# Twelve places in SBUF for the weights' two parts: each ring buffer starts at its own byte within 128

## The chip, the cores and the metric

One core of one Trainium2 chip. The metric is the device time of one execution in microseconds; runs of the same kernel are compared by their medians.

## The reference

Two layers on one sequence of 256 positions and a width of 1024, all in float32. Each layer adds a mixer, an MLP and a gated embedding to the running sum `x`:

```python
for i in range(DEPTH):                      # DEPTH = 2
    if i % 2 == 0:                          # layer 0: dilated attention, 16 heads, 3 groups
        x = x + dilated_attention(rms_norm(x, a_norm), a_w_qkv, a_q_gain, a_k_gain, a_w_o)
    else:                                   # layer 1: mLSTM with up and down projection
        x = x + mlstm_mixer(rms_norm(x, b_norm), b_w_up, ..., b_w_down)
    x = x + jnp.square(jax.nn.relu(rms_norm(x, mlp_norm[i]) @ mlp_w1[i])) @ mlp_w2[i]
    gate = jax.nn.sigmoid(rms_norm(x, ple_norm[i]) @ ple_w_gate[i])
    x = x + gate * (p[i] @ ple_w_proj[i])
```

The weights are 138 pieces of 128 x 2048 float32 (1 MB each), read once.

## The kernel before

**Three products for one.** Weights and activations are each split into two float32r parts, h (rounded) and l (the rest), and each 128 x 128 tile of weights is multiplied three times: h by h, h by l, l by h. In the streams of the MLPs, gates and projections (`stream`) the weights are the stationary operand, loaded anew before every matmul, and 256 columns of activations move (lines 335, 336 and 337, in this order). In `qkv_block` it is the other way about: 128 columns of the activations are stationary and 512 columns of weights move (lines 503 to 505).

**The weights' way.** A unit of 1 MB is loaded by one DMA (`raw`, three buffers) four units ahead. `split` cuts it into four slots of 512 columns: ScalarE copies a slot to the high part `hi` (line 180), VectorE subtracts to get `lo` (line 181). Both go to rings of twelve buffers of 2048 bytes a partition, some eleven slots ahead of use. A slot is 12 matmuls of 256 columns, or 6 of 512. Slot number `4*u + c` runs on over all units, so it returns to the same buffer every twelve slots.

**The order of the streams.** 36 units of `qkv` with the attention between them, then by units: proj0 1, woA and woB 4, w1_0 16, w2_0 16, gate0 4, xm 8, z0 to z3 8, wd0 4, proj1 1, wd1 4, w1_1 16, w2_1 16, gate1 4; 102 units of 48 matmuls of 256 columns. Small matmuls of attention and mLSTM (`fill`) stand between slots.

**Where the operands lie.** A pool's tiles stand one after another, each rounded up to 32 bytes (the 16-byte tile `rx` takes 32), and pools stand one after another; SBUF is full to its last hundred bytes in the mLSTM. The layout of the program before, as the byte of a partition's address within 128 at which a tile starts:

| tile | byte | it is read in |
|---|---|---|
| all twelve `hi`, all twelve `lo` | 64 | all streams |
| `raw` | 0 | splitting |
| `hA` (`hh`, `hl`), `hW` | 0 | qkv, w1_0, xm, z, wd1, gate1 |
| `hid` (`hidh`, `hidl`) of both MLPs, `hB` | 0 | w2_0, w2_1, w1_1, wd0 |
| `oT` (`oTh`, `oTl`) | 64 | woA, woB |
| `hG` (`hGh`, `hGl`), `pT` of layer 0, `x` | 96 | gate0, proj0 |
| `pT` of layer 1 | 32 | proj1 |

Weights and moving operand are thus 64 bytes apart in most streams, 0 in woA and woB, 96 (or -32) in gate0 and proj0, and 32 in proj1. The two lines `gap0` and `gap1` of 64 bytes make the weights' 64.

Of the kernel before, what the change touches and what calls it, by code (L numbers as in the profile page):

```python
# [10 lines left out]
F32 = mybir.dt.float32  # L11
F32R = mybir.dt.float32r
I32 = mybir.dt.int32
AF = mybir.ActivationFunctionType
# [4 lines left out]
D, S, P = 1024, 256, 128  # L19
# [9 lines left out]
UC = 2048  # L29
HU = 512  # L30
# [102 lines left out]
def build(tc, a):  # L133
    nc = tc.nc
    ctx = ExitStack()
    with ctx:
        _build(ctx, tc, nc, a)


def _build(ctx, tc, nc, a):  # L140
    def pool(n, b=1, c=ctx, **k):
        if "space" not in k:
            k["reuse_waits"] = "tile"
        return c.enter_context(tc.tile_pool(name=n, bufs=b, **k))

    base = pool("base")
    rawp = pool("raw", 3)

    pool("gap0").tile([P, 16], F32, name="gap0")
    hip, lop = pool("hi", 3 * UC // HU), pool("lo", 3 * UC // HU)  # L150
    pool("gap1").tile([P, 16], F32, name="gap1")
    psa = pool("psa", 3, space=PSUM)
    pst = pool("pst", 2, space=PSUM)
    pss = pool("pss", 2, space=PSUM)
# [3 lines left out]
    act = nc.scalar.activation  # L158
# [4 lines left out]
    raw, hi, lo = {}, {}, {}  # L163
# [6 lines left out]
    def split(u, c, back=None):  # L170
        if u >= NU:
            return
        n = u, c * 512 // HU
        if c * 512 % HU == 0:
            hi[n] = hip.tile([P, HU], F32R, name="hi")
            lo[n] = lop.tile([P, HU], F32R, name="lo")
        s = slice(c * 512, c * 512 + 512)
        d = slice(c * 512 % HU, c * 512 % HU + 512)
        with tc.high_priority(offset=-(BACK if back is None else back)):
            act(hi[n][:, d], raw[u][:, s], AF.Copy)  # L180
            dve.tensor_tensor(lo[n][:, d], raw[u][:, s], hi[n][:, d], op=ALU.subtract)  # L181
# [31 lines left out]
    def open_slot():  # L213
        u, c = divmod(clock[0], 4)
        while ahead[0] < clock[0] + lead[0]:
            ahead[0] += 1
            split(*divmod(ahead[0], 4))
        if c == 0:
            dma(u + LD)
        return u, c  # L220
# [11 lines left out]
    ones = base.tile([P, P], F32, name="ones")  # L232
# [6 lines left out]
                nc.sync.dma_start(x[:, 2 * j:2 * j + 2], a["x"][:, 2 * j:2 * j + 2])  # L239
            nc.sync.dma_start(raw[u][:, j * 512:(j + 1) * 512], a["w"][u, :, j * 512:(j + 1) * 512])  # L240
    nc.sync.dma_start(ident, a["eye"])
    first = base.tile([P, 1], F32, name="first")
    act(first, ones[:, 0:1], AF.Exp)

    warm = psm.tile([P, 512], F32, name="sm")
    for _ in range(WARM):
# [5 lines left out]

    hA = [base.tile([P, KT, S], F32R, name=f"h{n}") for n in "hl"]
    sqp = pool("sq", 2)

    class Stats:

# [25 lines left out]
    def rsqrt(y, v, shape):  # L283
        t = sqp.tile(shape, F32, name="rt")
        dve.tensor_scalar(y.bitcast(I32), v.bitcast(I32), -0.5, RSQRT_MAGIC, op0=ALU.mult, op1=ALU.add)
        for _ in range(3):
            dve.tensor_tensor(t, y, y, op=ALU.mult)
            dve.scalar_tensor_tensor(t, t, -0.5, v, op0=ALU.mult, op1=ALU.mult)
            dve.scalar_tensor_tensor(y, t, 1.5, y, op0=ALU.add, op1=ALU.mult)
# [62 lines left out]
    atp = pool("attn", c=actx)  # L352
# [5 lines left out]
    for j in range(4):  # L358
        for k in (2 * j, 2 * j + 1):
            scaled(hA, k, x[:, k], pr("gA"))  # L360
        split(0, j, 0)
    for j in range(4):
        split(1, j, 0)
# [13 lines left out]

    def first_stats():
        st.total()
        sw = atp.tile([P, P], F32, name="sw")  # L380
        dve.tensor_copy(sw[:, 0:64], st.s[:, 192:256])
        dve.tensor_copy(sw[:, 64:128], st.s[:, 0:64])
        for n, t in ((2, st.s[:, 64:192]), (3, sw)):
            mm(st.ps[:, 256 + n:257 + n], t, ones[:, 0:1], start=True, stop=True)
        v = atp.tile([P, 4], F32, name="v4")
        dve.tensor_scalar(v, st.ps[:, 256:260], 1.0 / D, EPS, op0=ALU.mult, op1=ALU.add)
        dve.tensor_scalar(epsx, v[:, 0:2], EPS, None, op0=ALU.mult)
        rsqrt(rx, v, [P, 4])

    def wrap():  # L390
        for n in range(2):
            act(hW[n][:, :, 0:64], hA[n][:, :, 192:256], AF.Copy)
            act(hW[n][:, :, 64:128], hA[n][:, :, 0:64], AF.Copy)

    at(0, first_stats)
    at(8, wrap)

# [283 lines left out]
    mp = pool("mlp0", c=mctx)  # L681
    hid = [mp.tile([P, 32, S], F32R, name=f"hid{n}") for n in "hl"]
# [11 lines left out]
    mp = pool("gate0", c=mctx)  # L694
# [279 lines left out]

    mctx = ExitStack()
    mp = pool("mlp1", c=mctx)
    hid = [mp.tile([P, 32, S], F32R, name=f"hid{n}") for n in "hl"]
    gst = Stats()
    mlp(1, x, hB, mst, hid, mp, hA, "gP1", gst)

# [98 lines left out]
```

## Time and profile before

| | |
|---|---|
| median of three runs | 910.12 us (909.98 to 912.25) |
| the profiled execution's own time | 912.26 us |
| its span, first to last instruction | 910.5 us |
| mean granted clock of TensorE | 0.997 of 2.4 GHz |
| TensorE busy, weight loads busy | 894.8 us (98%), 833.9 us (92%) |
| VectorE busy, ScalarE busy | 659.2 us (72%), 568.5 us (62%) |
| HBM read | 148 MB, 164 GB/s over the span |

Matmuls are pipelined, so the time of one (280 ns for 256 columns) is not what it adds to the span. What it adds is the distance between its start and the next one's, called its spacing below: in the timeline, where every matmul has a row, it is the last start less the first, divided by the rows between.

### The profile page before, as it was taken

The numbers are of one execution on the slowest core, as the hardware profiler recorded it, in microseconds if no ns is written. First come the engines' busy times: TensorE is split into PE (matmuls) and PEld (weight loads), VectorE is DVE, ScalarE is ACT, GpSimd is POOL, SyncE is SP. The second block draws the span as 40 slices with busy tenths as digits, with TensorE's granted clock in tenths as the row PEclk, the third lists the DMA queues.
The fourth block names the chain that finished last, engine by engine and source line by source line (L and its number), as shares of the span: only waits on it lengthen the run. The fifth ranks groups of instructions, "written<-read, shape, count | busy, mean of one in ns | idle before, by whom it ended". The sixth has DMA issues, their size and how long they took to land.

```text
span 910.5 us, 17609 instructions
## 1 busy us (share of the span) xinstructions
PE 894.8 (98%) x6924; PEld 833.9 (92%) x6924; DVE 659.2 (72%) x1409; ACT 568.5 (62%) x1055; POOL 39.4 (4%) x77
## 2 busy tenths in 40 slices
PE   8799999999999999999999999999999999999997
PEld 7687787777889999999999989999999999999997
DVE  6966877857876977765666987668898766656664
ACT  7567576676675766655555777678766666655552
POOL 0410000000000000000000343000000000000000
PEclk9999999999999999999999999999999999999999
DMA  8744434445343455555555433442256555555521
GB/s 305 282 140 147 178 130 150 143 141 180 132 148 137 149 188 185 190 183 188 187 191 175 154 130 134 140 140 93 94 197 223 175 187 188 188 183 188 190 102 47
DMA packets 23122, 150.23 MB, mean 165 GB/s; under 512 B 2560, under 2 KB 3200, under 8 KB 5632
## 3 DMA queue, kind: packets, MB, share of 16 engines
q1 hardware_dynamic: 23040, 149.12, 47.4%
q8 instruction: 54, 0.88, 0.4%
q14 instruction: 28, 0.23, 0.1%
HBM read 148.06 MB, written 1.05 MB: 164 GB/s over the span
## 4 chain that ended last, share of the span: by engine, by line
PE 92%; DVE 6%; issue 1%; ACT 1%; DMA 0%; SPq 0%; ACTq 0%
PE acc L335 21%; PE acc L336 21%; PE acc L337 20%; PE acc L503 6%; PE acc L505 6%; PE acc L504 6%; DVE lo L181 2%; PE tp L455 1%; PE tp L556 1%; PE sm L574 1%; PE sc L531 1%; PE tp L745 1%; PE tp L755 1%; PE sc L886 1%; PE sc L763 1%
## 5 line engine op out<-in xcount | busy, mean ns | idle before, releaser
L181 DVE TENSOR_TENSOR lo<-raw,hi 128x512 fp32r<-128x512 f32 x552 | 375.3, 690 | 169.2 <-ACT hi L180 163.8
L180 ACT ACTIVATE hi<-raw 128x512 fp32r<-128x512 f32 x552 | 338.7, 628 | 216.8 <-PE acc L336 194.1
L335 PE MATMUL acc<-hh,hi 128*128 128x256 f32 x640 | 182.5, 285 | 0.2 <-ACT hh L302 0.2
L336 PE MATMUL acc<-hl,hi 128*128 128x256 f32 x640 | 179.8, 281 | 0.4 <-DVE hl L303 0.3
L337 PE MATMUL acc<-hh,lo 128*128 128x256 f32 x640 | 179.7, 281 | 0.0
L337 PE MATMUL acc<-hidh,lo 128*128 128x256 f32 x512 | 143.3, 280 | 0.0
L336 PE MATMUL acc<-hidl,hi 128*128 128x256 f32 x512 | 143.3, 280 | 0.0
L335 PE MATMUL acc<-hidh,hi 128*128 128x256 f32 x512 | 143.1, 279 | 0.0
L336 PEld LDWEIGHTS acc<-hl,hi 128*128 128x128 f32 x640 | 121.7, 190 | 1.0 <-DVE hl L303 0.8
L335 PEld LDWEIGHTS acc<-hh,hi 128*128 128x128 f32 x640 | 120.7, 189 | 1.5 <-issue 0.7
L337 PEld LDWEIGHTS acc<-hh,lo 128*128 128x128 f32 x640 | 120.3, 188 | 0.0
L503 PE MATMUL acc<-hi,hh 128*128 128x512 f32 x264 | 109.9, 417 | 0.0
L504 PE MATMUL acc<-lo,hh 128*128 128x512 f32 x264 | 104.4, 396 | 0.8 <-DVE lo L181 0.8
L505 PE MATMUL acc<-hi,hl 128*128 128x512 f32 x264 | 104.8, 397 | 0.0
L336 PEld LDWEIGHTS acc<-hidl,hi 128*128 128x128 f32 x512 | 96.3, 188 | 0.0
L335 PEld LDWEIGHTS acc<-hidh,hi 128*128 128x128 f32 x512 | 96.2, 188 | 0.0
L337 PEld LDWEIGHTS acc<-hidh,lo 128*128 128x128 f32 x512 | 96.0, 188 | 0.0
L336 PE MATMUL acc<-hBl,hi 128*128 128x256 f32 x320 | 89.9, 281 | 0.0
L335 PE MATMUL acc<-hBh,hi 128*128 128x256 f32 x320 | 89.8, 281 | 0.0
L337 PE MATMUL acc<-hBh,lo 128*128 128x256 f32 x320 | 89.5, 280 | 0.0
L335 PEld LDWEIGHTS acc<-hBh,hi 128*128 128x128 f32 x320 | 60.3, 188 | 0.3 <-issue 0.3
L336 PEld LDWEIGHTS acc<-hBl,hi 128*128 128x128 f32 x320 | 60.1, 188 | 0.0
(258 smaller groups left out, 1382.7 us busy)
## 6 DMA issues: line engine op xcount, KB each, us to landing
raw<-w SPq DMA_DIRECT2D x136, 1024.0 KB, 4.9
raw<-w SPq DMA_DIRECT2D x8, 256.0 KB, 5.9
x<-x SPq DMA_DIRECT2D x4, 256.0 KB, 5.6
pj<-rep SPq DMA_DIRECT2D x1, 896.0 KB, 6.7
out<-u SPq DMA_DIRECT2D x3, 256.0 KB, 2.4
pT<-p SPq DMA_DIRECT2D x2, 256.0 KB, 3.9
nd<-nd SPq DMA_DIRECT2D x1, 384.0 KB, 5.6
out<-u SPq DMA_DIRECT2D x2, 128.0 KB, 1.9
```

The costliest lines, as they stand in the source:

```text
L180: act(hi[n][:, d], raw[u][:, s], AF.Copy)
L181: dve.tensor_tensor(lo[n][:, d], raw[u][:, s], hi[n][:, d], op=ALU.subtract)
L335: mm(acc[:, q], wh, h, start=first, stop=False, skip_group_check=n > 1)
L336: mm(acc[:, q], wh, l, start=False, stop=False, skip_group_check=n > 1)
L337: mm(acc[:, q], wl, h, start=False, stop=last, skip_group_check=n > 1)
L455: nc.tensor.transpose(ps[:, pair, b * P:(b + 1) * P], n[:, b, ty * 256 + pair * P:ty * 256 + (pair + 1) * P], ident)
L503: mm(accs[b], hh, wh, start=(k == 0), stop=False)
L504: mm(accs[b], hh, wl, start=False, stop=False)
L505: mm(accs[b], hl, wh, start=False, stop=(k == 7))
L531: mm(ps[:, 0:256], q[r, pair, tb], k[r, pair], start=first, stop=last)
L556: nc.tensor.transpose(psf[:, k * P:(k + 1) * P], pe[:, k * P:(k + 1) * P], ident)
L574: mm(out, VT[qt, 0][:, n, cols], pt[:, n * P:(n + 1) * P], start=(n == 0), stop=False, skip_group_check=True)
```

## The change

The two pools of twelve buffers become 24 pools of one buffer, with gap tiles between them, so that the buffers of a ring no longer start at one byte within 128. `RING` lists the intended pairs (byte of `hi`, byte of `lo`), counted from the end of `raw`; slot n uses pair n modulo 12. In the second MLP a gap of 32 bytes is put between `hidh` and `hidl`. To make room, the tile `first` (4 bytes, a slot of 32) goes: the early `Exp`, which has ScalarE load its table, now writes a tile `v` of the pool `sq` and stands after the warm-up matmuls in the program; and `sw` (512 bytes) takes the place of `t2` by a common tag.

```diff
-    pool("gap0").tile([P, 16], F32, name="gap0")
-    hip, lop = pool("hi", 3 * UC // HU), pool("lo", 3 * UC // HU)
-    pool("gap1").tile([P, 16], F32, name="gap1")
+    RING = ((64, 64), (64, 0), (64, 32), (64, 96), (0, 64), (32, 32), (96, 96), (32, 96), (96, 32), (48, 48), (80, 80), (0, 0))
+    ring = {}
+    at_ = 0
+    for part in range(2):
+        for n in sorted(range(len(RING)), key=lambda n: RING[n][part]):
+            gap = (RING[n][part] - at_) % 128
+            if gap:
+                pool(f"gap{part}{n}").tile([P, gap // 4], F32, name="gap")
+            at_ += gap
+            ring[part, n] = pool(("hi", "lo")[part] + str(n))
+    pool("gap").tile([P, (-at_) % 128 // 4], F32, name="gap")
...
-            hi[n] = hip.tile([P, HU], F32R, name="hi")
-            lo[n] = lop.tile([P, HU], F32R, name="lo")
+            hi[n], lo[n] = (ring[part, (4 * u + c) % len(RING)].tile([P, HU], F32R, name=nm) for part, nm in enumerate(("hi", "lo")))
...
-    first = base.tile([P, 1], F32, name="first")
-    act(first, ones[:, 0:1], AF.Exp)
...
     sqp = pool("sq", 2)
+    act(sqp.tile([P, 2], F32, name="v"), ones[:, 0:2], AF.Exp)
...
-        sw = atp.tile([P, P], F32, name="sw")
+        sw = atp.tile([P, P], F32, name="sw", tag="t2")
...
-    hid = [mp.tile([P, 32, S], F32R, name=f"hid{n}") for n in "hl"]
+    hid = []
+    for n in "hl":
+        if n == "l":
+            mp.tile([P, 8], F32, name="gap")
+        hid.append(mp.tile([P, 32, S], F32R, name=f"hid{n}"))
```

## Rows read from the trace of the kernel before

**Rows 1.** The page: busy time by engine, and the chain that ended last.

```profile
PE 894.8 (98%) x6924; PEld 833.9 (92%) x6924; DVE 659.2 (72%) x1409; ACT 568.5 (62%) x1055; POOL 39.4 (4%) x77
...
PE 92%; DVE 6%; issue 1%; ACT 1%; DMA 0%; SPq 0%; ACTq 0%
```

**Rows 2.** Busy time by stretch: us, then each engine's busy us and instructions.

```profile
100.00:200.00 100.00, 100.00 (x662) 79.85 (x659) 73.02 (x190) 65.06 (x134) 0.00 (x0) 1.00 0.43 148
...
400.00:450.00 50.00, 50.00 (x427) 50.00 (x426) 29.98 (x49) 24.97 (x42) 0.00 (x0) 1.00 0.54 182
```

**Rows 3.** TensorE's waits: who waited for whom, total us, times, longest.

```profile
PE tp L455 <- DVE nqk L447: 4.9, 1, 4.9
...
PE acc L504 <- DVE lo L181: 0.8, 1, 0.8
```

**Rows 4.** TensorE's timeline in w2_0, first and last of 147 matmuls.

```profile
409.76 0.28 PE L335 MATMUL acc<-hidh,hi 128*128 128x256 f32 x1
...
426.96 0.28 PE L337 MATMUL acc<-hidh,lo 128*128 128x256 f32 x1
```

**Rows 5.** The same in z1 (27 matmuls) and in z3 (26 matmuls).

```profile
594.00 0.28 PE L335 MATMUL acc<-hh,hi 128*128 128x256 f32 x1
...
597.07 0.28 PE L337 MATMUL acc<-hh,lo 128*128 128x256 f32 x1
...
627.11 0.28 PE L336 MATMUL acc<-hl,hi 128*128 128x256 f32 x1
...
629.95 0.28 PE L337 MATMUL acc<-hh,lo 128*128 128x256 f32 x1
```

**Rows 6.** The same in woB, 26 matmuls.

```profile
299.83 0.28 PE L336 MATMUL acc<-oTl,hi 128*128 128x256 f32 x1
...
302.83 0.28 PE L337 MATMUL acc<-oTh,lo 128*128 128x256 f32 x1
```

**Rows 7.** The same in gate0, two stretches: 26 and 97 matmuls.

```profile
486.22 0.28 PE L336 MATMUL acc<-hGl,hi 128*128 128x256 f32 x1
...
489.22 0.28 PE L337 MATMUL acc<-hGh,lo 128*128 128x256 f32 x1
...
497.17 0.28 PE L337 MATMUL acc<-hGh,lo 128*128 128x256 f32 x1
...
508.37 0.28 PE L337 MATMUL acc<-hGh,lo 128*128 128x256 f32 x1
```

**Rows 8.** The same in proj1, 37 matmuls.

```profile
673.47 0.29 PE L337 MATMUL acc<-pT,lo 128*128 128x256 f32 x1
...
677.73 0.28 PE L337 MATMUL acc<-pT,lo 128*128 128x256 f32 x1
```

**Rows 9.** The same in qkv, 512 columns: 25 matmuls, and 8 with hW.

```profile
191.43 0.40 PE L505 MATMUL acc<-hi,hl 128*128 128x512 f32 x1
...
196.92 0.39 PE L505 MATMUL acc<-hi,hl 128*128 128x512 f32 x1
...
73.59 0.40 PE L505 MATMUL acc<-hi,hWl 128*128 128x512 f32 x1
...
75.23 0.39 PE L503 MATMUL acc<-hi,hWh 128*128 128x512 f32 x1
```

**Rows 10.** Groups by line: busy us, mean ns; idle before, releaser.

```profile
L181 DVE TENSOR_TENSOR lo<-raw,hi 128x512 fp32r<-128x512 f32 x552 | 375.3, 690 | 169.2 <-ACT hi L180 163.8
...
L654 DVE TENSOR_TENSOR hidl<-s,hidh 128x512 fp32r<-128x512 f32 x32 | 22.2, 693 | 3.2
```

**Rows 11.** DMA issues: times, KB each, median us to landing.

```profile
raw<-w SPq DMA_DIRECT2D x8, 256.0 KB, 5.9
x<-x SPq DMA_DIRECT2D x4, 256.0 KB, 5.6
```

**Rows 12.** ScalarE's first instructions.

```profile
0.73 1.28 ACT L243 ACT_TABLE_LOAD   x1 [0.73 <-PEq L1071]
...
5.05 0.91 ACT L302 ACTIVATE hh<-x,prm 128x256 fp32r<-128x256 f32 x2 [2.83 <-DMA x<-x]
```

## The prediction

> **What bounds the kernel now.** I read the page first. TensorE's matmuls cover 98% of the span and the chain that ended last is 92% PE [rows 1]; the longest wait of TensorE for another engine is 4.9 us, the one for a weight part 0.8 us [rows 3]. So the end is set by how fast matmuls follow each other, and VectorE, ScalarE and the DMA queue matter only where they would make TensorE wait. A busy share of 98% hides the quantity that counts here, so I went to the timeline and took spacings: last start less first start, by the rows between. In w2_0 it is (426.96 - 409.76) / 146 = 117.8 ns [rows 4]; the window 400 to 450 us holds 427 matmuls, 50 us / 427 = 117.1 ns [rows 2], less by the matmuls in flight at its ends.
>
> The reader is to compare spacings of one and the same instruction, 128 x 128 weights and 256 moving columns, in different streams:
>
> - weights and moving operand 64 bytes apart: 117.8 ns [rows 4], but also 3.07 / 26 = 118.1 ns in z1 and 2.84 / 25 = 113.6 ns in z3, with the same tiles [rows 5];
> - 0 apart (`oT`): 3.00 / 25 = 120.0 ns [rows 6];
> - 96 apart (`hG`): first 3.00 / 25 = 120.0 ns, after a break in the stream 11.20 / 96 = 116.7 ns [rows 7];
> - 32 apart (`pT` of proj1): 4.26 / 36 = 118.3 ns [rows 8].
>
> At 2.4 GHz, the clock granted nearly everywhere, 256 columns are 106.7 ns; every stream pays 7 to 13 ns on top. In qkv, 512 columns (213.3 ns) take 5.49 / 24 = 228.8 ns, and 1.64 / 7 = 234.3 ns with `hW` [rows 9]. What goes with the differences is the place of the operands; and since one place gives two values (z1, z3), also a state into which a stream falls and in which it stays until something breaks it: w2_0 holds its 117.8 ns through 147 rows.
>
> The Trainium skill speaks against any such effect: "TensorE: Matmul & The Clock Gate", in "Step-by-step: what each phase is for", says that matmul and weight load read SBUF through two independent ports and that loading the next weights takes no read bandwidth from the running matmul; "SBUF — State Buffer", under "Who interferes with whom", that PE waits for nobody there. By that rule the change is worth 0. The trace does not agree, by 113.6 against 120.0 ns for one shape at one clock [rows 5, 6].
>
> **Which places the change really gives.** A slot of a pool is rounded up to 32 bytes, so the gaps of 16 bytes before the entries 48, 64, 80 and 96 take 32 each. I count the layout through. `first` gives back 32 bytes, so `hh`, `raw` and the start of the ring move to 96 within 128, and the activations with them; only distances can matter if anything does. By slot the pairs (`hi`, `lo`) become, from that start: (96,32), (96,64), (96,96) twice, (0,32), (32,96) four times, (64,0), (0,64) twice. So `hi` lies at 0 three times, at 32 four, at 64 once, at 96 four times; `lo` at 0 once, 32 twice, 64 three times, 96 six times. The pair (64,64) of before is gone. If the 16-byte gaps are taken as written instead, the twelve pairs of the list hold; the mean below moves by some 0.2 ns, within the bounds.
>
> **The streams of 256 columns.** A price for each distance, from the rows: 120.0 at 0; 118.3 at 32; at 96 the mean over its two stretches, (25 x 120.0 + 96 x 116.7) / 121 = 117.4; at 64 the middle of 117.8 and 113.6, 115.7, since a slot of twelve matmuls between two others may land in either state. Of three matmuls two run beside the loading of a `hi` tile and one beside a `lo` tile. Mean for `hi`: (3 x 120.0 + 4 x 118.3 + 115.7 + 4 x 117.4) / 12 = 118.2. For `lo`: (120.0 + 2 x 118.3 + 3 x 115.7 + 6 x 117.4) / 12 = 117.3. A triple: (2 x 118.2 + 117.3) / 3 = 117.9 ns. That prices add in this way when the distance changes inside a triple is not shown by any row; it is my choice between the ends below.
>
> - 76 units (w1, w2, wd, gate1; 3648 matmuls) are at 117.8 now: +0.1 ns, +0.4 us.
> - 16 units (xm, z; 768) are some at 113.6, some at 118.1 now [rows 5], middle 115.9: +2.0 ns, +1.5 us.
> - woA and woB (192) are at 120.0; `oT` lies 64 from the others, so each price moves on by 64: (2 x 117.5 + 118.4) / 3 = 117.8: -0.4 us.
> - gate0, proj0, proj1 (288), at 117.4 to 118.3 now: +0.1 us.
> - The second MLP's gap shifts the distance of `lo` to `hidl` by 32 in a third of w2_1, 256 matmuls: `lo` would stand at 117.2 for 117.3: nothing.
>
> Sum +1.6 us. Ends: all 4896 matmuls at 113.6 would be -15.3 - 1.8 - 1.2 - 1.1 = -19 us; all at 120.0 would be 8.0 + 3.1 + 0.7 = +12 us.
>
> **The qkv streams.** 864 matmuls, 48 of them with `hW`. The same distance of 64 bytes shows 228.8 and 234.3 ns [rows 9], so here distance within 128 alone does not tell the price. Ends: 0, and 816 x 5.5 ns = +4.5 us. I take a fifth of that, +0.9 us, since nearly all of qkv runs at the lower value now.
>
> **The other edits.** VectorE's subtraction is 690 ns with `raw` at 0 and `hi` at 64 and 693 ns for the same operation with both inputs at 0 [rows 10]: its place costs nothing, and both splitting engines idle behind TensorE anyway (busy 72% and 62%). `raw` moves to an address of 32 within 64; `x` lies so already, and its DMA of 256 KB lands in 5.6 us against 5.9 for `raw`'s [rows 11]: nothing, with a 1 MB load issued four units (over 20 us) ahead as cover; were it gone, each unit would wait for its load. The early `Exp` keeps its place as ScalarE's first instruction: the table load ends at 2.0 us, and the next instruction waits for `x` until 5.05 us [rows 12]; without that cover it would cost 1.3 us. `sw` is last read long before `t2` is written by slot 52: nothing. Buffers are handed back one by one as before, twelve slots apart: no new wait.
>
> **Sum.** +1.6 + 0.9 = +2.5 us. On the profiled execution's own 912.26 us that is 914.8; on the median of the runs, 910.12, which lies 2.1 us below it, 912.6 us. A measurement of this kernel can tell some 0.3%, 2.7 us, from no change, so the forecast stands at the edge between the same and slower.
>
> **Rivals.**
>
> - *The held state breaks (the other side).* Place: the 3648 matmuls that stand at 117.8 in undisturbed streams. Now nothing disturbs them; after, the distance jumps every twelve matmuls and inside each triple. In xm and z, where small matmuls break the stream, z3 sits at 113.6 [rows 5], and gate0 fell from 120.0 to 116.7 after breaks [rows 7]. Against it: z1 stayed at 118.1 between breaks, and 113.6 is seen only at a distance of 64, which few buffers keep. Price: at 115.7 everywhere -2.1 x 3648 = -7.7 us, 902.5; in full -15 us, 895. It decides once the mean of the ring is below 117.1 ns (-0.7 x 3648 = -2.7 us).
> - *Jumps cost more than any one place.* Then most slots go to 120 ns: +12 us, 922; with qkv at its upper end 926. At half of it 917. For it: 120.0 stands wherever distance is 0, and the ring holds three such `hi`. Against: no stream shows more than 120.0 for long.
> - *The places do not matter in sum, or the change does not do what it says:* within 1 us, 910 to 911. For it: distances 32, 64 and 96 all average 116 to 118 ns.
>
> **How the numbers follow.** My forecast's case, a mean of 117.4 to 118.6 ns and so -1 to +6 us, gets 0.5; its own range is 909 to 916. The held state breaking gets 0.25, dearer jumps 0.15, no effect 0.1. Slower by over 0.3%: half of the first case and the third, 0.41; faster: 0.25; the rest, 0.34, within. The range leaves out the far half of the second case and the far end of the third: 903 to 919.
>
> **What would show it.** Take the spacing by slot in w1 and w2: right is a pattern that returns every twelve slots, between some 114 and 120 ns, slots with `hi` and the moving tile 0 apart the slowest; a window of 50 us in w2 holds 426 to 428 matmuls again. Wrong would be one flat value in all slots, or slots under 113 or over 121. The xm and z streams should lose their runs at 113.6 ns. DMA, the subtraction's 690 ns and the start should stay. The prediction fails if the prices do not add across a triple: then the mean can lie anywhere between 113.6 and 120.

## The result, and the profile after

The changed kernel takes 917.17 us (916.25 to 917.49, three runs) against 910.12 for the one before: 1.0074 times as long [1.0056, 1.0091], slower by 7.05 us. Its profiled execution took 916.25 us with a span of 914.4 us against before's 910.5; unrounded it is 914.45 against 910.45, 4.0 us more. So of the 7 us between the medians a little over half stands in the two traces; the rest lies between the runs of either kernel and is taken up below. Two executions of the kernel before in later sessions, of 1093 and 4981 us, are slow ones and are left out everywhere.

The page of the changed kernel, busy time and the chain that ended last:

```profile
PE 899.2 (98%) x6924; PEld 836.8 (92%) x6924; DVE 659.9 (72%) x1409; ACT 569.5 (62%) x1055; POOL 41.5 (5%) x77
...
PE 95%; DVE 4%; ACT 1%; DMA 1%; issue 0%; SPq 0%; ACTq 0%
```

TensorE has 4.4 us more of busy time for the same 6924 matmuls [rows 1]. Its waits did not grow; the two that answer to [rows 3]:

```profile
PE tp L461 <- DVE nqk L453: 4.8, 1, 4.8
...
PE acc L510 <- DVE lo L188: 0.7, 1, 0.7
```

The subtraction did not grow either (690 ns before [rows 10]), and the 136 loads of 1 MB land in 4.9 us both times. Only the loads of 256 KB at the start land a little later than in [rows 11], 6.2 for 5.9 us (6.8 in a second trace of before):

```profile
L188 DVE TENSOR_TENSOR lo<-raw,hi 128x512 fp32r<-128x512 f32 x552 | 375.9, 691 | 171.6 <-ACT hi L187 166.8
...
raw<-w SPq DMA_DIRECT2D x136, 1024.0 KB, 4.9
raw<-w SPq DMA_DIRECT2D x8, 256.0 KB, 6.2
x<-x SPq DMA_DIRECT2D x4, 256.0 KB, 5.7
```

What is left is the spacing of the matmuls. Busy time by stretch, in qkv and in w2_0: 10 matmuls fewer in 100 us and 2 fewer in 50 us than in [rows 2], at a granted clock of 1.00 both times (the prediction had 426 to 428 in w2; it is 425).

```profile
100.00:200.00 100.00, 100.00 (x652) 79.25 (x653) 73.14 (x189) 64.57 (x133) 0.00 (x0) 1.00 0.43 148
400.00:450.00 50.00, 50.00 (x425) 50.00 (x424) 29.73 (x48) 25.04 (x42) 0.00 (x0) 1.00 0.53 182
```

TensorE's timeline of the changed kernel, first and last row of four stretches that answer to [rows 4, 5, 6, 9]: qkv (25 matmuls), woB (32), w2_0 (146), z3 (17).

```profile
192.04 0.39 PE L511 MATMUL acc<-hi,hl 128*128 128x512 f32 x1
...
197.61 0.39 PE L511 MATMUL acc<-hi,hl 128*128 128x512 f32 x1
...
298.73 0.28 PE L343 MATMUL acc<-oTh,lo 128*128 128x256 f32 x1
...
302.35 0.28 PE L341 MATMUL acc<-oTh,hi 128*128 128x256 f32 x1
...
409.73 0.27 PE L343 MATMUL acc<-hidh,lo 128*128 128x256 f32 x1
...
426.89 0.28 PE L341 MATMUL acc<-hidh,hi 128*128 128x256 f32 x1
...
630.78 0.28 PE L342 MATMUL acc<-hl,hi 128*128 128x256 f32 x1
...
632.68 0.28 PE L343 MATMUL acc<-hh,lo 128*128 128x256 f32 x1
```

Read as spacings: qkv 5.57 / 24 = 232.1 ns (228.8 before), woB 3.62 / 31 = 116.8 (120.0), w2_0 17.16 / 145 = 118.3 (117.8), z3 1.90 / 16 = 118.8 (113.6; over all of z3 it is 118.2 against 113.9). The same for whole stages, from the starts of all their matmuls; the means leave out pauses over 135 ns (280 in qkv), and the lengths run from a stage's first matmul to that of the next:

| stage | mean before, ns | mean after, ns | length before, us | length after, us | more, us |
|---|---|---|---|---|---|
| start to w1_0 (qkv, attention, woA, woB) | 229.9 in qkv | 232.2 in qkv | 302.98 | 303.89 | 0.91 |
| w1_0 | 117.78 | 118.04 | 91.58 | 91.75 | 0.17 |
| w2_0 | 117.78 | 118.33 | 90.46 | 90.88 | 0.42 |
| gate0 to wd1 | | | 215.44 | 217.03 | 1.59 |
| of that: xm | 115.15 | 118.11 | 70.12 | 70.55 | 0.43 |
| of that: z0 to z3 | 115.2 | 118.0 | 64.87 | 65.78 | 0.91 |
| w1_1 | 117.78 | 118.32 | 91.35 | 91.78 | 0.43 |
| w2_1 | 117.78 | 118.12 | 90.45 | 90.71 | 0.26 |
| gate1 to the end | 116.96 | 118.18 | 28.19 | 28.41 | 0.22 |

They add up to 4.0 us, spread thinly over every stage. 0.3 us of it came before qkv's first matmul, for which the first piece of weights landed later; in the rest no wait or transfer has a share.

By slot, the changed kernel shows the pattern that was forecast: it returns every twelve slots, and from the second round on w2_0 and w1_1, whose tiles lie alike, agree in each slot within 0.1 ns. It is not in the order forecast. Worked out from the program's layout (distance = byte of the weights less byte of the moving tile, here already counted within 256, for which see the experiments) and from the starts:

```
slot                   0     1     2     3     4     5     6     7     8     9    10    11
hi to hid, bytes     224   224   224   224   128   160    32   160    32   192     0   128
lo to hid, bytes     160    64    96   224   160    96   224   224    96   128   192    64
mean in w2_0, ns   117.7 119.2 118.8 117.9 118.2 119.0 118.5 119.5 117.9 117.4 117.6 118.2
```

The slots with `hi` 0 apart within 128 (4, 10, 11) take 118.2, 117.6 and 118.2 ns; the slowest is slot 7.

### The profile page after: what moved, and what is told of

It reads as the page before. It is cut to its first block, busy times and chain, and to the rows that moved or that the text cites. A ratio compares the mean times of both kernels' runs of the same rounds, so it can differ in the third digit from the quotient of the medians.

```text
span 914.4 us, 17608 instructions
## 1 busy us (share of the span) xinstructions
PE 899.2 (98%) x6924; PEld 836.8 (92%) x6924; DVE 659.9 (72%) x1409; ACT 569.5 (62%) x1055; POOL 41.5 (5%) x77
## 4 chain that ended last, share of the span: by engine, by line
PE 95%; DVE 4%; ACT 1%; DMA 1%; issue 0%; SPq 0%; ACTq 0%
PE acc L341 21%; PE acc L342 21%; PE acc L343 20%; PE acc L509 7%; PE acc L510 7%; PE acc L511 7%; PE tp L461 1%; PE tp L562 1%; PE sm L580 1%; PE sc L537 1%; DVE lo L188 1%; PE tp L751 1%; PE tp L761 1%; PE sc L892 1%; PE sc L769 1%; PE sc L543 1%
## 5 line engine op out<-in xcount | busy, mean ns | idle before, releaser
L511 PEld LDWEIGHTS acc<-hi,hl 128*128 128x128 f32 x264 | 50.0, 189 | 11.8
```

Of the source, the lines that this page charges most:

```text
L511: mm(accs[b], hl, wh, start=False, stop=(k == 7))
```

## The experiments

The theory was: the distance in bytes between stationary and moving operand sets the spacing, together with a state into which a stream falls. Rivals: the places do nothing and another edit costs the time; or it is the jumps from place to place that cost.

**1. One place for all twelve (e1_all64).** The changed kernel with every other edit kept:

```diff
-    RING = ((64, 64), (64, 0), (64, 32), (64, 96), (0, 64), (32, 32), (96, 96), (32, 96), (96, 32), (48, 48), (80, 80), (0, 0))
+    RING = ((64, 64),) * 12
```

> The changed kernel with all twelve pairs of the ring set to (64,64): the 24 pools, the shifted base, the moved Exp, the shared sw and the gap in the second hid stay, the ring of places goes. Theory (distance between weights and moving operand sets the spacing, and a stream of one distance holds a state): w1 and w2 go back to one flat spacing, 117.8 ns (or 113.6), and the time to 909 to 912.5 us. Rival (the pools, the address of raw or the other edits cost the time): the streams keep some 118.2 ns or wait, and the time stays at 916 to 917.5 us.

Measured: 913.30 us (912.54 to 914.94), 1.0023 [1.0011, 1.0034] of before, which took 910.84 in the same session; that is 0.8 us above the range expected. TensorE's timeline, w2_0 (147 matmuls) and w2_1 (146):

```profile
409.79 0.28 PE L343 MATMUL acc<-hidh,lo 128*128 128x256 f32 x1
...
426.99 0.28 PE L342 MATMUL acc<-hidl,hi 128*128 128x256 f32 x1
...
804.77 0.28 PE L343 MATMUL acc<-hidh,lo 128*128 128x256 f32 x1
...
821.93 0.28 PE L341 MATMUL acc<-hidh,hi 128*128 128x256 f32 x1
```

w2_0 is back at 17.20 / 146 = 117.8 ns, and w1_0, w1_1 and qkv (229.9) with it: the twelve places made these streams slower, though the time did not come back whole (points 2 and 6). w2_1 stands at 17.16 / 145 = 118.3 although its weights have one place now: there the moving tile `hidl` is shifted by the 32-byte gap.

**2. The same without the gap in the second MLP (e5_all64_nogap).**

```diff
+    RING = ((64, 64),) * 12
...
-        if n == "l":
-            mp.tile([P, 8], F32, name="gap")
```

> The changed kernel with all twelve pairs at (64,64) and without the gap in the second hid: only the 24 pools, the base shifted by 32 bytes, the moved Exp and the shared sw are left of the change. Theory (only distances cost): w2_1 at 117.8 or 113.6 ns flat, where the run with the gap had 118.3, and the time within 1 us of the kernel before of the same call. Rival (the other edits cost some 2 us): 912.5 to 913.5 us.

Measured: 912.83 us (912.43 to 914.40), 1.0019 [1.0007, 1.0031]; w2_1 returns to 117.78 ns (121 matmuls, 14.14 / 120 = 117.8):

```profile
799.77 0.28 PE L343 MATMUL acc<-hidh,lo 128*128 128x256 f32 x1
...
813.91 0.28 PE L343 MATMUL acc<-hidh,lo 128*128 128x256 f32 x1
```

So the gap costs 768 x 0.55 ns = 0.4 us when the weights have one place. The time lies in the rival's range: against before's median the ring machinery, the moved `Exp` and `sw` still cost a fifth of a per cent, with every run at 912.4 or above; before itself has runs on both sides of that (point 6). The trace shows nothing of it in the streams: from w1_0 to the end e5 takes 607.25 us, before 607.47, before's second trace (point 6) 607.45, the changed kernel 610.56. What e5's trace is longer by stands ahead of w1_0, which starts at 304.56 us for 302.98; there the mean granted clock from 40 to 60 us is 0.83 in e5 and 0.91 in before.

**3. One place, 0 apart (e2_all0).**

```diff
+    RING = ((0, 0),) * 12
```

> The changed kernel with all twelve pairs at (0,0): one distance everywhere, as in the kernel before, but 0 instead of 64. Theory: the spacing of w1, w2, wd, gate, xm and z is 120.0 ns as in woB before, woB itself (now 64 apart) 117.8 or 113.6; against the kernel before +2.2 ns x 3648 = +8.0 us, about +4.8 ns x 768 = +3.7 us in xm and z, -0.4 us in woA and woB, and in qkv between 0 and +4.5 us: 922 to 926 us. Rival (what costs is the jump from one place to the next, not the place): without jumps as the kernel before, 910 to 912 us.

Measured: 922.07 us (921.41 to 922.50), 1.0118 [1.0103, 1.0134]. Windows, then TensorE's timeline in woB (46 matmuls) and w2_0 (144):

```profile
400.00:450.00 50.00, 50.00 (x419) 50.00 (x418) 29.52 (x48) 24.61 (x41) 0.00 (x0) 1.00 0.54 184
```

```profile
297.31 0.28 PE L341 MATMUL acc<-oTh,hi 128*128 128x256 f32 x1
...
302.41 0.28 PE L341 MATMUL acc<-oTh,hi 128*128 128x256 f32 x1
...
409.73 0.28 PE L343 MATMUL acc<-hidh,lo 128*128 128x256 f32 x1
...
426.89 0.28 PE L342 MATMUL acc<-hidl,hi 128*128 128x256 f32 x1
```

419 matmuls in 50 us instead of 427, 17.16 / 143 = 120.0 ns in w2_0, and in woB, which was at 120.0 with 0 apart and is now 64 apart, 5.10 / 45 = 113.3. The places alone, with no jumps at all, move the kernel by 9 us against e1 (922.07 to 913.30). The rivals that places do not matter, and that jumps are what costs, fall for the streams of 256 columns. qkv does not follow their list: 229.1 ns here, where the place of 0 is no dearer than that of 64 (229.9).

**4. Twelve pairs without the rounding (e6_ring32).** The list asks for 48 and 80, which become 64 and 96 and push later entries on; here all entries are multiples of 32:

```diff
-    RING = ((64, 64), (64, 0), (64, 32), (64, 96), (0, 64), (32, 32), (96, 96), (32, 96), (96, 32), (48, 48), (80, 80), (0, 0))
+    RING = ((64, 64), (64, 0), (64, 32), (64, 96), (0, 64), (32, 32), (96, 96), (32, 96), (96, 32), (0, 32), (32, 0), (0, 0))
```

> The changed kernel with twelve different pairs, all multiples of 32 bytes, so that no gap is rounded up: the list as it stands, with (48,48) and (80,80) replaced by (0,32) and (32,0). Theory (a ring pays about the mean of its distances): 118.0 to 118.3 ns in w1 and w2, 915 to 918 us, as the changed kernel. Rival (the rounding, which put four slots on one pair and dropped (64,64), made the change slow): under 117 ns, 910 us or less.

Measured: 917.41 us (916.89 to 918.96), 1.0071 [1.0049, 1.0093]; w1_0 118.17, w2_0 118.15, w2_1 118.39 ns. TensorE's timeline in w2_0 (147 matmuls, 17.26 / 146 = 118.2):

```profile
409.49 0.28 PE L342 MATMUL acc<-hidl,hi 128*128 128x256 f32 x1
...
426.75 0.28 PE L341 MATMUL acc<-hidh,hi 128*128 128x256 f32 x1
```

In the same session e5, with one place, took 912.83 us. The loss comes from spreading the weights over many places; that pairs fell together by rounding does not matter. Pairs that are truly 16 bytes apart were not tried.

**5. Breaking a held stream (e3_kick, e9_kick32).** In the kernel before, two small float32 matmuls into an idle buffer, once in w1_0 and once in w1_1; in e9 their stationary operand is a copy of `ident` that starts at 32 within 128:

```diff
+        def kick():
+            ps = pst.tile([P, 2, S], F32, name="tp")
+            for i in range(2):
+                mm(ps[:, i], ident, pj[:, i], start=True, stop=True)
+
+        at(clock[0] + 8, kick)
```

> The kernel before with two float32 matmuls of 256 columns into an unused PSUM tile, once in w1_0 and once in w1_1, at their ninth slot; their output is never read. Theory (117.8 and 113.6 ns are two states of one distance, kept until the stream is broken; after such float32 matmuls xm and z mostly went on at 113.6): from there to the end of w2 some 1420 matmuls in each layer run at 113.3 to 113.6 ns, 2840 x 4.3 = -12 us, less 2 x 0.5 us for the break: 899 us. Rival (the spacing belongs to the stream, its tiles or what else runs beside it): 117.8 ns goes on, and the time is 911 us.

> As e3_kick, the kernel before with two float32 matmuls once in w1_0 and once in w1_1, but their stationary operand is a copy of the identity that starts at byte 32 within 128 and their moving operand at 0, as the float32 matmuls at line 755 of the kernel before have them, after which xm and z went on at 113.3 ns six times of six (e3_kick had the stationary operand at 96, and 117.8 ns followed). Theory (which of its two states a stream takes is set by how it is broken, and it keeps it): 113.3 ns from the kick to the end of w2 in both layers, some 1420 matmuls each, 2840 x 4.4 = -12.5 us, less 2 x 0.9 us: 900 to 902 us. Rival (the state after a break is chance): 911 to 915 us, as e3_kick.

Measured: e3 913.98 us (910.96 to 915.07), 1.0023 [1.0010, 1.0035]; e9 911.90 us (910.77 to 915.88), 0.9999 [0.9983, 1.0015]. Both miss the times expected, 899 and 900 to 902 us. But e3's timeline shows two states in one stream with the same tiles, w1_0 before the kick (25 matmuls) and after it (65):

```profile
311.39 0.28 PE L337 MATMUL acc<-hh,lo 128*128 128x256 f32 x1
...
314.11 0.28 PE L337 MATMUL acc<-hh,lo 128*128 128x256 f32 x1
...
319.45 0.28 PE L336 MATMUL acc<-hl,hi 128*128 128x256 f32 x1
...
326.99 0.28 PE L337 MATMUL acc<-hh,lo 128*128 128x256 f32 x1
```

2.72 / 24 = 113.3 ns, then 7.54 / 64 = 117.8. In e9, w1_0 stays at 113.39 ns to its end (126 matmuls after the kick, 14.16 / 125 = 113.3), and w2_0 begins at 117.78:

```profile
319.80 0.28 PE L337 MATMUL acc<-hh,lo 128*128 128x256 f32 x1
...
333.96 0.28 PE L336 MATMUL acc<-hl,hi 128*128 128x256 f32 x1
```

In both, w1_1 has 117.8 before the kick and after it. So w1_0 knows 113.3 and w1_1 does not, though both have 64 bytes between weights and moving operand within 128. They differ within 256: 64 in w1_0, 192 in w1_1 and w2.

**6. The kernel before once more (e10_before).** A copy, for a second trace.

> The kernel before once more, for a second trace of it. Its runs lie in two groups, near 910 and near 912.5 us; the profiled one was of the upper. Theory (a stream's state differs from run to run): in a run of the lower group w1_0 is at 113.3 ns from its start, 88.4 us long, where the first trace has 91.6; in one of the upper group both are alike. Rival (the groups come from the half-speed clock of the first 50 us alone): w1_0 is 91.6 us long in either.

Measured: 912.96 us. w1_0 begins at 113 ns and falls to 117.8 in its fifth slot; it is 91.58 us long again, as in the first trace, since the pause at the break is 0.2 us longer. The 75 runs of before in all sessions lie in two groups: 34 of 907.95 to 911.23 (mean 909.87) and 41 of 911.74 to 914.73 (mean 913.03), 3.15 us apart. The rival, the clock, does not tell the groups apart: over the 72 runs of the later sessions the mean granted clock is 0.995 in either. A w1_0 that keeps 113.4 ns is 88.40 us long (e7 and e12), 3.18 us less than 91.58. That fits the lower group, but both traces of before are of the upper one, so it is argued, not shown. The runs of e3 and e9 lie in two such groups as well; e9's trace, of its lower group, has w1_0 89.24 us long with the kick, e3's, of its upper, 92.20.

**7. Other distances (e4_hid, e7_places, e8_places).** In the kernel before, only activations moved, by gaps ahead of them; e4:

```diff
     mp = pool("mlp0", c=mctx)
+    mp.tile([P, 16], F32, name="gap")
...
     mp = pool("mlp1", c=mctx)
+    mp.tile([P, 24], F32, name="gap")
     hid = [mp.tile([P, 32, S], F32R, name=f"hid{n}") for n in "hl"]
```

> The kernel before with only the hidden tiles moved: in the first MLP hid by 64 bytes (distance 0 to the weights), in the second by 96 (distance -32, as hG in gate0). Theory: w2_0 at 120.0 ns flat (+1.7 us), w2_1 at 116.7 or 120.0 ns, w1_0 and w1_1 at 117.8 as before. Rival (places do not matter, or only those of the weights' ring do): both w2 at 117.8 ns.

The other two put such gaps ahead of the h and the l tile each, in bytes: `hid` of MLP 0 (0, 64), `hB` (32, 0), `hid` of MLP 1 (96, 96) in e7; (64, 64), (32, 96), (96, 32) in e8.

> The kernel before with moving tiles at other places, weights left at 64: distances (to the high part, to the low part) of (64,0) in w2_0, (64,96) in w2_1, (32,32) in w1_1 and wd0. Theory of prices that add: w2_0 at (2 x 117.8 + 120.0) / 3 = 118.5 ns (115.7 if the 64 is in its better state), w2_1 at 117.0 to 117.8, w1_1 at 118.3. Rival (a pair has a price of its own that its two distances do not give): any of them off by over 1 ns.

> The kernel before with moving tiles at other places, weights left at 64: distances (to the high part, to the low part) of (0,64) in w2_0, (96,64) in w2_1, (32,64) in w1_1 and wd0. Theory of prices that add: w2_0 at (2 x 120.0 + 117.8) / 3 = 119.3 ns (117.9 with the better state), w2_1 at 116.0 to 117.5, w1_1 at 116.7 to 118.1. Rival (a pair has a price of its own): any of them off by over 1 ns.

Measured, one run each: 916.65, 912.37 and 911.96 us. e4's timeline in w2_0 (144 matmuls, 128 apart within 256) and w2_1 (148, 96 apart):

```profile
409.79 0.29 PE L337 MATMUL acc<-hidh,lo 128*128 128x256 f32 x1
...
426.95 0.28 PE L336 MATMUL acc<-hidl,hi 128*128 128x256 f32 x1
...
799.74 0.28 PE L335 MATMUL acc<-hidh,hi 128*128 128x256 f32 x1
...
816.99 0.28 PE L335 MATMUL acc<-hidh,hi 128*128 128x256 f32 x1
```

17.16 / 143 = 120.0, as expected, and 17.25 / 147 = 117.3 ns, where 116.7 or 120.0 was expected. e8's timeline in w2_0 (142 matmuls; 128 from `hidh`, 64 from `hidl`):

```profile
409.83 0.29 PE L336 MATMUL acc<-hidl,hi 128*128 128x256 f32 x1
...
426.91 0.28 PE L336 MATMUL acc<-hidl,hi 128*128 128x256 f32 x1
```

17.08 / 141 = 121.1 ns, above either price. The streams that hold several distances, means over the stage, the distances to the h tile and to the l tile:

| stage | distances | measured, ns | adding single prices, ns |
|---|---|---|---|
| e7 w2_0 | 192, 128 | 117.8 | (2 x 117.8 + 120.0) / 3 = 118.5 |
| e7 w2_1 | 64, 224 | 120.0 | at most (2 x 117.8 + 120.0) / 3 = 118.5 |
| e7 w1_1 | 160, 160 | 120.0 | one distance |
| e8 w2_0 | 128, 64 | 121.1 | at most (2 x 120.0 + 117.8) / 3 = 119.3 |
| e8 w1_1 | 160, 64 | 118.5 | at most (2 x 120.0 + 117.8) / 3 = 119.3 |
| e8 w2_1 | 224, 192 | 117.8 | at most (2 x 120.0 + 117.8) / 3 = 119.3 |

e7's timeline in w2_1 (121 matmuls, 14.40 / 120 = 120.0):

```profile
799.49 0.28 PE L337 MATMUL acc<-hidh,lo 128*128 128x256 f32 x1
...
813.89 0.28 PE L337 MATMUL acc<-hidh,lo 128*128 128x256 f32 x1
```

The distances 64 and 224 have two prices, so the last column is an upper bound in four rows (the lower ones, with 113.3 at 64 and 116.7 at 224, are 114.4, 117.8, 117.8 and 117.1 for e7 w2_1 and the three rows of e8). Three rows lie outside what adding allows, by -0.7, +1.5 and +1.8 ns: prices do not add inside a held triple (one trace each), so the rival of both expectations holds. In e7 and e8 w1_0 keeps 113.4 ns throughout, 88.40 and 88.42 us long, with nothing changed in it.

**8. The distance of 64 within 256 (e11_dist64_kick, e12_dist64).** If it is the only one that knows 113.3 ns, the held streams have to be put there, and the change is two gaps in the kernel before, ahead of the first `hid` and of `hB` (MLP 1's `hid` moves along with `hB`):

```diff
     mp = pool("mlp0", c=mctx)
+    mp.tile([P, 32], F32, name="gap")
     hid = [mp.tile([P, 32, S], F32R, name=f"hid{n}") for n in "hl"]
...
+    xp1.tile([P, 32], F32, name="gap")
     hB = [xp1.tile([P, KT, S], F32R, name=f"hB{n}") for n in "hl"]
```

e11 has the kick of e9 besides.

> The kernel before with 128 bytes of gap ahead of hB and ahead of the first hid (the second hid moves along with hB), so that w1_1, w2_0, w2_1 and wd0 have the distance 64 within 256 that w1_0, xm and z have, instead of 192; and with the two float32 matmuls of e9_kick32 in w1_0 and w1_1. In all runs so far streams at 64 within 256 stood at 113.3 or 117.8 ns, and streams at 192 at 117.8 alone. Theory (the distance counts within 256 bytes, and 64 alone has the better state): 113.3 ns from the break to the end of w2 in both layers, 2840 x 4.4 = -12.5 us, less 1.9 us for the breaks: 900 to 903 us. Rival (192 and 64 are alike, the state was chance): w2_0, w1_1 and w2_1 at 117.8 again, 911 to 914 us.

> As e11_dist64_kick without the float32 matmuls: the kernel before with hB and both hid at the distance 64 within 256. Theory: each stream is at 113.3 or 117.8 ns by how the break before it left it, so runs between 899 and 913 us, the median below 910, and single traces with w1 or w2 whole at 113.3. Rival (192 and 64 are alike): w2_0, w1_1 and w2_1 at 117.8, the time as the kernel before.

Measured: e11 911.52 us (six runs of 907.37 to 909.50, six of 913.54 to 915.56), 1.0002 [0.9980, 1.0025], a miss against 900 to 903; e12 905.42 us (904.36 to 908.12), 0.9931 [0.9910, 0.9953] of before's 912.27 in that session. Windows of e12 in w2_0 and in w2_1, and TensorE's timeline in w2_0 (152 matmuls):

```profile
400.00:450.00 50.00, 50.00 (x444) 50.00 (x443) 32.12 (x53) 26.29 (x44) 0.00 (x0) 1.00 0.59 193
750.00:800.00 50.00, 50.00 (x427) 50.00 (x426) 34.11 (x53) 29.82 (x51) 0.00 (x0) 1.00 0.54 184
```

```profile
409.83 0.28 PE L337 MATMUL acc<-hidh,lo 128*128 128x256 f32 x1
...
426.94 0.28 PE L335 MATMUL acc<-hidh,hi 128*128 128x256 f32 x1
```

444 matmuls in 50 us, 17.11 / 151 = 113.3 ns: w2_0 is 87.04 us long for 90.46, w1_0 88.40 for 91.58, wd1 21.78 for 22.61. w2_1 at the same distance stands in the other state, 427 matmuls and 117.78 ns, and w1_1 falls from 113.3 to 117.8 ns after its third slot (35 matmuls before the fall, 3.85 / 34 = 113.2, and 35 behind it, 4.01 / 34 = 117.9):

```profile
694.46 0.28 PE L336 MATMUL acc<-hBl,hi 128*128 128x256 f32 x1
...
698.31 0.28 PE L337 MATMUL acc<-hBh,lo 128*128 128x256 f32 x1
698.43 0.50 PE L276 MATMUL sm<-ones,ssum 128*128 128x1 f32 x4
698.99 0.28 PE L336 MATMUL acc<-hBl,hi 128*128 128x256 f32 x1
...
703.00 0.28 PE L337 MATMUL acc<-hBh,lo 128*128 128x256 f32 x1
```

The fall stands at the small float32 matmuls of the statistics (lines 276 and 297), and so does every lasting change of state of w1_0 and w1_1 in these traces, if not at the kick: w1_0 of e10 falls at line 276, that of e5 at 297 (303 there), that of e11 falls at 276 and rises again at 297; w1_0 of e7 and e12 passes both unchanged.

The span of e12 is 903.7 us, 6.8 less than before's. Only w2_0's 3.4 us belong to a tile that was moved. w1_0 (3.2) and wd1 (0.8) lie where they lay and were in the better state in this trace, as w1_0 seems to be in before's lower group; against that group's mean e12 gains 4.5 us. This version is faster than both kernels, and two stages of 768 matmuls, w1_1 (91.19 us) and w2_1 (90.45), still stand some 3 us above the lengths of w1_0 and w2_0.

## Why the prediction was right or wrong

The time, 917.17 us, lies in the range, on the slower side that had the highest chance, and 4.6 us above the 912.6 forecast. It lies outside the 909 to 916 of the forecast's own case and on the 917 that the prediction gave for half of the rival *jumps cost more*; what decides for the forecast's case is the trace, with w1 and w2 at 118.0 to 118.3 ns (117.4 to 118.6 said) and 4.0 us more (-1 to +6 said). That the median came out so high is in part the luck of before's three runs, as told below.

**Layout: right.** The program's layout gives the pairs as counted. e6 shows that the rounded list and an unrounded one cost the same.

**Mechanism: right; distances moved the spacing.** e2 against e1 shows it alone, and the waits, the subtraction and the loads of 1 MB stood still. The rule of the Trainium skill that spoke against it ("TensorE: Matmul & The Clock Gate", "Step-by-step: what each phase is for": loading the next weights takes no read bandwidth from the running matmul) does not hold here: with only `hid` moved, w2_0 runs at 120.0 ns in e4 and at 113.3 ns in e12, while the splitting engines write to the same places as before.

**The term that was mis-sized: the 76 units held at 117.8.** "+0.1 ns, +0.4 us" became +0.2 to +0.6 ns a matmul and +1.6 us in the trace (w1_0 0.17, w2_0 0.42, w1_1 0.43, w2_1 0.26, wd0 0.10, wd1 0.03, gate1 0.22). The step that failed is the price for each distance within 128. The bytes count within 256: 64 and 192, one entry at 115.7 in the list, are 113.3 or 117.8 and 117.8 alone; 32 and 160, one entry at 118.3, are 118.4 and 120.0. With the list of the last section (118.4 for 32, the middle of 115.5 for 64, gate0's mean before of 117.5 for 224) the same sum over the slots gives 118.4 ns for w2_0 (measured 118.33) and 118.2 for w1_0 (118.04). As a mean over twelve slots adding was good enough; slot by slot it was not, and the sentence that `hi` at 0 would be slowest failed, by 117.6 to 118.2 ns for those slots against 119.5 in slot 7.

**The other terms.** xm and z: +1.5 forecast, +1.3 measured (0.43 + 0.91), and the runs at 113.6 ns were lost, as said (z3 118.2). woA and woB: -0.4 forecast, -0.17 measured. qkv: +0.9 forecast, +0.7 us in its stretch; its matmuls are 2.3 ns dearer, nearer the middle of the two ends than to a fifth; 816 times that would be 1.9 us, so most of it did not lengthen the stretch, which has pauses, and the nearness of 0.9 and 0.7 is in part luck. w2_1's gap was put at nothing; by e1 it costs 0.4 us with one place. gate0 and the projections: +0.1 forecast, +0.2. The remaining 0.3 us came before qkv's first matmul, where the prediction had the start unchanged. Two slips of the prediction change nothing: the first three matmuls of its stretch in z1 still belong to z0, and half of its first case and the third make 0.40, not 0.41. On the profiled executions 914.8 was forecast and 916.25 came.

**The median.** Of the 4.6 us above the forecast 1.5 are those terms, 0.9 the step from the profiled execution to the median of after, and 2.1 the choice to carry the sum over to before's median of three. Before's runs have two groups 3.15 us apart, the profiled execution (912.26) belongs to the upper and two of the three runs to the lower; the changed kernel's runs keep within 1.2 us. Against the median of all 75 runs of before, 912.1, the change costs 5.1 us, and e6, the other ring, lies 4.6 us above e5 in one session. So it seems that the change also takes away the runs in which, as argued in experiment 6, w1_0 keeps 113.4 ns: e1 and e5, at one place, stay in the upper group as well (912.4 to 914.9), so this part is not due to the spread of places. What in the shared edits decides it is open.

**The rivals.** *The held state breaks* fell: no slot without a pause came under 116.6 ns in w1 and w2, and the distance that knows 113.3 is rare in the ring. *Jumps cost more* fell for the streams of 256 columns: 118.3 ns with jumps in every slot, less than the 120.0 of e2 with none, and the sum of single prices, 118.4, leaves nothing over for them. For qkv it stands untested: one place gives 229.1 or 229.9 ns, the two rings 232.2 and 231.9, and no run tells the jumps from the distances that only the rings have. *The places do not matter* fell by e2.

**Open:** what repeats after 256 bytes; by what a break puts a stream at distance 64 into one state or the other; why triples with two distances do not add; what makes qkv dearer with a ring; the lower group of before, of which there is no trace. Experiment 8 shows where a stream changes its state, not what decides it.

## What to carry to other kernels

Where matmuls with freshly loaded weights fill the time, compare the spacing of equal matmuls between stages, from starts in the timeline: at 98% busy, 113 and 120 ns look alike. Then hold the byte distance between stationary and moving operand, counted within 256 and after the rounding of tiles to 32, at the one value that the fastest stage has, for all buffers; spreading a ring over many places buys the average. Even then part of the streams can stay at 117.8 ns, as w1_1 and w2_1 of e12 did. Take the time of before from enough runs to see whether it has two groups, before a profiled execution is set against a median.

## What the runs showed of the hardware

Spacing of float32r matmuls of 128 x 128 by 256 columns, weights loaded for each, at the 2.4 GHz level, by weights' byte less moving byte within 256:

| distance | spacing, ns | seen in |
|---|---|---|
| 0 | 120.0 | woB before; w1, w2, wd1 of e2 |
| 32 | 118.1 to 118.5 | proj1 before, proj0 of e2 |
| 64 | 113.3 or 117.8 | w1_0 of e3 (both); w2_0 (113.3) and w2_1 (117.8) of e12; woB of e2 (113.3) |
| 96 | 117.3 | w2_1 of e4, proj1 of e2 |
| 128 | 120.0 | w2_0 of e4 |
| 160 | 120.0 | w1_1 and wd0 of e7 |
| 192 | 117.8 | w2_0, w2_1, w1_1 before |
| 224 | 120.0, then 117.8, later 116.7 | gate0 before [rows 7]; 116.7 throughout in e12 |

A state holds through hundreds of matmuls (768 in w2_0 of e12) until small matmuls break the stream (experiment 8). The clock had a part in the spread of single runs: in the windows from 40 to 60 us the mean granted clock is 0.91 before and after but 0.83 in e1, e2, e4, e5, e10 and e12, and from 0 to 20 us 0.83 in e4 and 0.91 in e1 against 1.00 in the others named; with levels of 2.4 and 1.2 GHz, 0.83 of 20 us is 6.8 us at the lower one. From 40 to 60 us TensorE was busy for 15.2 us of 20 in before. The lower clock is part of e4's 916.65 us (mean clock 0.991), of which w2_0 itself accounts for 1.7.
